# Eight taps per convolution column of the second token half: from VectorE to ScalarE and accumulating DMAs of GpSimd

## Chip, cores and metric

The kernel runs on one NeuronCore of a Trainium2 chip. The metric is the device time of one execution in microseconds; the median of three runs of the kernel before is 3363.21 us (3360.95 to 3363.67).

## What is computed

The reference is a stack of transformer blocks on 1024 tokens of width 1024. Only the first mixer matters here. Its first branch makes `a_val * sigmoid(a_gate)` (512 channels), puts it through a causal depthwise convolution of 31 taps, a layer norm and a SiLU; the second branch is a gated linear recurrence; both are joined and multiplied by `w_out`:

```python
CONV_WIDTH = 31
ya = jax.nn.silu(layer_norm(causal_depthwise_conv(a_val * jax.nn.sigmoid(a_gate), conv_w, conv_b),
                            cnorm_g, cnorm_b))
yb = rg_lru(causal_depthwise_conv(b_rec, lru_conv_w, lru_conv_b), w_a, b_a, w_x, b_x, lru_lambda) \
    * jax.nn.gelu(b_gate)
return jnp.concatenate([ya, yb], axis=-1) @ w_out
```

After it come a layer norm, a SwiGLU feed-forward, differential attention with its own feed-forward, and a second block (mLSTM and Fourier mixing, another feed-forward). Everything is float32; a matrix product is done as three products of a high and a low part.

## The kernel before

Activations lie with channels on the 128 partitions and tokens along the free dimension. The 512 channels of the first branch are four **columns** c of 128 channels; the 1024 tokens are two **halves** h of 512. For column c, `ga[c]` holds the gated values and `co[c]` the convolution's sum, both 128 x 1024 float32 in SBUF.

`mixer_even` (L411) goes through the columns. `a_proj(c)` (L459) multiplies the weights on TensorE, ScalarE takes the gate from PSUM through a sigmoid (L463) and VectorE multiplies the value in (L466). `conv(c, h)` (L481) is the convolution of one half: ScalarE begins it with tap 0 and the bias (L483), then 30 VectorE instructions (L487) each add one shifted, scaled copy of `ga[c]` to `co[c]` in place. For half 0 these are 511 to 482 elements long, for half 1 always 512. In the same loop (L549 to L558) `r_proj`, `taps` (L506) and `lru` (L509) make the recurrence of column c; `lru` multiplies on TensorE (L515) into two PSUM buffers that ScalarE empties with sigmoids (L516). The loop calls `conv(c, 0)` for each column, but the second halves, `conv(c, 1)`, stand only after the pipeline of the first four token tiles (L630 to L632).

That pipeline is `prep0` (L573: transpose the four `co` columns of a tile of 128 tokens on TensorE, L576; mean and variance on VectorE; the inverse root on GpSimd, L261 and L262; normalise on VectorE, L579), `prep1` (L581: transpose back, L584; SiLU on ScalarE, L587) and the products with `w_out` (L592, L565). A second pipeline (L634) does tiles 4 to 7, which need the second halves of all four columns, and starts the feed-forward (`start`, L770).

The order on each engine is not the order of the calls. A list scheduler fixes it when the kernel is built: it takes at each moment the instruction called earliest among those whose inputs and buffers are ready by its cost estimates. So second-half taps, called late, are put as fill into VectorE's free moments from the start. At run time each engine goes through its own list strictly in order and waits where an input isn't there. Buffers come from pools; `self.tmp` (L204) gives 128 x 512 buffers of which there are three, and a fourth waits until the first was released by its last reader. GpSimd issues no DMA in the kernel before; all are issued on SyncE's queue.

Of the kernel before, what the change touches and what calls it, by code (L numbers as in the profile page):

```python
# [14 lines left out]
ALU = mybir.AluOpType  # L15
AX = mybir.AxisListType
P = 128
S = 1024
# [3 lines left out]
H512 = 512  # L22
# [32 lines left out]
TS, TS0, TSM, T2 = True, False, True, 3  # L55
SE, SO, S2, S3, S4 = 1, 0, 1, 0, 1
NC1 = 0
EY = 2
W0 = 0
HA = 1  # L60
# [25 lines left out]
def half(h):  # L86
    return slice(h * H512, (h + 1) * H512)


def blk(i):  # L90
    return slice(i * P, (i + 1) * P)
# [70 lines left out]
class Net:  # L162
# [248 lines left out]
    def mixer_even(self, xr, xn, start):  # L411
        nc, A = self.nc, self.A
# [3 lines left out]
        for h in range(2):  # L416
            r = self.rp.tile([P, KT, P], F32, tag="raw", name=self.name("raw"))
            w0.append([self.wp.tile([P, KT, P], F32R, tag="w", name=self.name("w0")) for _ in range(2)])
            for k in range(0, KT, 2):
# [4 lines left out]
                t = self.u("xt", (P, 2, H512))  # L424
# [28 lines left out]
        ga = [self.u("ga") for _ in range(4)]  # L453
        co = [self.u("co") for _ in range(4)]
# [4 lines left out]
        def a_proj(c):  # L459
            g = ga[c]  # L460

            def gate(p, h):
                nc.scalar.activation(g[:, half(h)], p, AF.Sigmoid, bias=self.c("b_in", 4 + c))  # L463

            def val(p, h):
                nc.vector.scalar_tensor_tensor(g[:, half(h)], p, self.c("b_in", c), g[:, half(h)],  # L466
                                               op0=ALU.add, op1=ALU.mult)

            if c > 0:
                proj(4 + c, gate)  # L470
                yield
                proj(c, val)
                return
            yield
            for h in range(2):
                for w, evac in zip(w0, (gate, val)):
                    p = self.pa("pi")
                    self.feat(p, w, x, h)
                    evac(p, h)

        def conv(c, h):  # L481
            lo_, hi_ = h * H512, (h + 1) * H512
            nc.scalar.activation(co[c][:, lo_:hi_], ga[c][:, lo_:hi_], AF.Identity, bias=self.c("conv_b", c),  # L483
                                 scale=self.c("conv_w", 31 * c + 30))
            for s in range(1, 31):
                a = max(lo_, s)
                nc.vector.scalar_tensor_tensor(  # L487
                    co[c][:, a:hi_], ga[c][:, a - s:hi_ - s], self.c("conv_w", 31 * c + 30 - s),
                    co[c][:, a:hi_], op0=ALU.mult, op1=ALU.add)

        def r_proj(c):
            rec = recs[c] = self.u("rec")

            def evr(p, h):
                nc.scalar.activation(rec[:, half(h)], p, AF.Identity, bias=self.c("b_in", 12 + c))

            proj(12 + c, evr)
# [3 lines left out]
        def taps(c):  # L501
            rec = recs[c]
            rc = rcs[c] = self.u("rc")
            nc.scalar.activation(rc, rec, AF.Identity, bias=self.c("lconv_b", c), scale=self.c("lconv_w", 4 * c + 3))
            for s in range(1, 4):
                nc.vector.scalar_tensor_tensor(rc[:, s:], rec[:, :S - s], self.c("lconv_w", 4 * c + 3 - s),  # L506
                                               rc[:, s:], op0=ALU.mult, op1=ALU.add)

        def lru(c):  # L509
            rec, rc = recs[c], rcs[c]  # L510
            r, ig, a = self.u("r"), self.u("ig"), self.u("a")
            for h in range(2):
                for j, (dst, b) in enumerate(((r, "b_a"), (ig, "b_x"))):
                    p = self.pb("pg")[:, 0:H512]
                    nc.tensor.matmul(p, wg[:, 4 * j + c, :], rc[:, half(h)], start=True, stop=True)  # L515
                    nc.scalar.activation(dst[:, half(h)], p, AF.Sigmoid, bias=self.c(b, c))  # L516
            nc.scalar.activation(a, r, AF.Exp, scale=ca[:, 4 + c:5 + c])
            nc.scalar.activation(r, r, AF.Tanh, scale=ca[:, c:c + 1])
            nc.vector.tensor_mul(ig, ig, rc)
            nc.scalar.activation(rc, a, AF.Square)  # L520
            nc.vector.scalar_tensor_tensor(r, rc, 1.0, r, op0=ALU.add, op1=ALU.mult)
            nc.scalar.activation(r, r, AF.Sqrt)
            nc.vector.tensor_mul(ig, ig, r)
            nc.vector.tensor_tensor_scan(rec, a, ig, 0.0, op0=ALU.mult, op1=ALU.add)
# [3 lines left out]
        def g_steps(cs):  # L528
            ws = [self.weight(A["w_in0"][8 + c], pool=8 + c in W0P) for c in cs]
            gs = [self.u("gel") for c in cs]  # L530
            for h in range(2):
                for c, w, g in zip(cs, ws, gs):
                    p = self.pa("pi")
                    self.feat(p, w, x, h)
                    nc.scalar.activation(g[:, half(h)], p, AF.Gelu_apprx_tanh, bias=self.c("b_in", 8 + c))
                    if h == 1:
                        nc.vector.tensor_mul(g, g, recs[c])
                        hi, lo = self.u("ybh", dt=F32R), self.u("ybl", dt=F32R)
                        self.split(hi, lo, g)
                        yb.append((hi, lo))  # L540
                    yield

        def run(g):
            for _ in g:
                pass

        run(a_proj(0))
        conv(0, 0)
        for c in range(4):  # L549
            r_proj(c)  # L550
            taps(c)
            g = a_proj(c + 1) if c < 3 else g_steps((0,))
            if EV:
                next(g, None)
            lru(c)
            run(g)
            if c < 3:
                conv(c + 1, 0)  # L558
        def rows_b(p, i, first, last):
            for h in range(2):  # L560
                for c in range(4):
                    self.mm3(p[:, half(h)], (yb[c][0][:, blk(i)], yb[c][1][:, blk(i)]),
                             (wb[0][:, c, half(h)], wb[1][:, c, half(h)]), first and c == 0, last and c == 3)

        def prod_b(i):  # L565
            p = self.pb("yo")
            rows_b(p, i, True, True)
            nc.vector.scalar_tensor_tensor(xr[i], xr[i], DN_ALPHA, p, op0=ALU.mult, op1=ALU.add)
# [38 lines left out]

        for c in range(NC1):
            conv(c, 1)
# [20 lines left out]
        self.pipe(pre + [(2, prod_ab), (2, lambda i: prod_b(i + 4)), (3, norm)], range(4))  # L630
        for c in range(NC1, 4):
            conv(c, 1)  # L632
# [698 lines left out]
    def block2_mix(self, x, xr, xn, start):  # L1331
# [370 lines left out]
        def gather(i):  # L1702
            og = self.u("og", (P, 4, P))
            nc.sync.dma_start(og, ogd[:, :, blk(i)].rearrange("h p t -> p h t"))
            if i < 4:
                yf = [[yfs[k // 2][l][:, k % 2, blk(i)] for k in range(4)] for l in range(2)]
            else:
                t = self.y_tile()
                for a in range(2):
                    self.split(*(t[l][:, 2 * a:2 * a + 2, :] for l in range(2)), y2s[a][:, :, blk(7 - i)][:, :, ::-1])  # L1710
                yf = [[t[l][:, k, :] for k in range(4)] for l in range(2)]
            ys[i] = [yf, og, None]

        def prod_f(i):
            p, y = self.pb("yo"), ys[i][0]
            ys[i][2] = p
            for h in range(2):
                for k in range(4):
                    self.mm3(p[:, half(h)], (y[0][k], y[1][k]),
                             (w[0][0][:, k, half(h)], w[0][1][:, k, half(h)]), k == 0, False)  # L1720
                    if k % 2:
                        yield
# [7 lines left out]
        def early():  # L1730
            for _ in fg:
                yield
            w.append(self.load_w_out(A["w_out2"], 4))
            for i in range(EY):
                gather(i)
            yield
            for i in range(EY):
                yield from prod_f(i)
# [16 lines left out]
        def moments(i):  # L1755
            if i >= EY:
                gather(i)
            mv = self.small("mv4", 8)
            m3 = mv.rearrange("p (h t) -> p h t", t=2)
            hh = [H[h // 2][i // 4][:, i % 4, (h % 2) * P:(h % 2 + 1) * P] for h in range(4)]  # L1760
            for h in range(4):
                st = self.mp.tile([P, 6], F32, tag="bn4", name=self.name("st"), bufs=4)
                nc.vector.bn_stats(st, hh[h])
                nc.vector.bn_aggr(m3[:, h, :], st)
            rs = self.small("rs4", 4)
            self.rsqrt(rs, m3[:, :, 1], 1.0, EPS)
            nm = self.small("nm4", 4)
            nc.vector.scalar_tensor_tensor(nm, m3[:, :, 0], -1.0, rs, op0=ALU.mult, op1=ALU.mult)
            ys[i].append((nm, rs, hh))
            xr.append(self.u("xr"))  # L1770
            nc.sync.dma_start(xr[i], spill[blk(i), :])
# [258 lines left out]
```

## Time and profile before

| | us |
|---|---|
| median of 3 runs | 3363.21 |
| the profiled execution, its own time | 3360.71 |
| its span (first to last instruction) | 3358.9 |
| TensorE (PE) busy | 3245.6 |
| VectorE (DVE) busy | 2195.7 |
| ScalarE (ACT) busy | 1389.4 |
| GpSimd (POOL) busy | 226.3 |

PE is matmul, DVE VectorE, ACT ScalarE, POOL GpSimd, SP SyncE. Times in rows count from the start of the span. A timeline merges like instructions that follow each other: a row gives start, length, instruction, tile written <- tiles read, how many, and in brackets the idle time before it with what ended it. A waits row says who waited for whom, the total, the count and the longest. A stretch row gives the stretch, its length, and per engine the busy time with the number of instructions. Line numbers are those of the kernel before.

### The profile page before, as it was taken

Reading aid. Unit: us, or ns where it says so; the run is one execution under the profiler, and the core shown is the slowest. Engines: PE = TensorE matmul, PEld = TensorE weight load, DVE = VectorE, ACT = ScalarE, POOL = GpSimd, SP = SyncE. Lnnn points to the kernel's source line nnn. Section 1 sums busy time; section 2 is a strip of 40 time slices with the busy share of each in tenths; the row PEclk is TensorE's granted clock in tenths of the full one; section 3 lists DMA queues with packets and bytes.
Section 4 is the critical chain, followed back from the end, with each engine's and each line's share of the span. In section 5 each row is a group of like instructions: output and inputs, shape, how many; then the busy total and the mean of one; then the engine's idle time right before and its main releaser. Section 6 shows DMA issues by size and latency. Waiting matters only on the chain. (4 is left out here: it accounts for less than half of the span.)

```text
span 3358.9 us, 40965 instructions
## 1 busy us (share of the span) xinstructions
PE 3245.6 (97%) x15588; PEld 2688.4 (80%) x15588; DVE 2195.7 (65%) x3474; ACT 1389.4 (41%) x2402; POOL 226.3 (7%) x417
## 2 busy tenths in 40 slices
PE   8998999999999999999999999999999999999998
PEld 7777788888878888877788888788777878888887
DVE  8998855555457777676765558654346986675535
ACT  4554433332137777663533331234335454442111
POOL 1011000000010111111000000023001200000001
PEclk9999999999999999999999999999999999999999
DMA  3131322234222111151332238621123333354312
GB/s 127 44 113 63 108 87 76 91 130 161 84 74 98 54 32 51 41 157 60 119 110 91 99 131 296 200 89 68 57 76 116 110 129 118 112 183 161 105 50 80
DMA packets 191765, 348.69 MB, mean 104 GB/s; under 512 B 14384, under 2 KB 105936, under 8 KB 191568
## 3 DMA queue, kind: packets, MB, share of 16 engines
q1 hardware_dynamic: 191568, 346.07, 31.0%
q8 instruction: 123, 2.02, 0.2%
q14 instruction: 74, 0.61, 0.1%
HBM read 268.41 MB, written 72.36 MB: 101 GB/s over the span
## 5 line engine op out<-in xcount | busy, mean ns | idle before, releaser
L214 ACT CAST wh<-raw 128x1024 fp32r<-128x1024 f32 (+1 forms) x275 | 282.7, 1047 | 330.4 <-DVE raw L677 131.3
L215 DVE TENSOR_TENSOR wl<-raw,wh 128x1024 fp32r<-128x1024 f32 (+1 forms) x275 | 330.2, 1217 | 111.6 <-ACT wh L214 107.4
L214 ACT CAST ht<-ht 128x512 fp32r<-128x512 f32 (+1 forms) x168 | 97.2, 579 | 534.9 <-DMA ht<-hd 511.5
L236 PE MATMUL dn<-wd,ht 128*128 128x512 f32 x704 | 274.0, 389 | 0.8 <-ACT wd L214 0.8
L237 PE MATMUL dn<-wd,ht 128*128 128x512 f32 x704 | 274.0, 389 | 0.6 <-DVE wd L215 0.6
L238 PE MATMUL dn<-wd,ht 128*128 128x512 f32 x704 | 273.9, 389 | 0.0
L215 DVE TENSOR_TENSOR ht<-ht 128x512 fp32r<-128x512 f32 (+1 forms) x168 | 106.6, 638 | 171.4 <-ACT ht L214 170.3
L236 PE MATMUL dn<-wh,ht 128*128 128x512 f32 x512 | 201.6, 394 | 8.1 <-DVE xr L901 6.8
L238 PE MATMUL dn<-wh,ht 128*128 128x512 f32 x512 | 200.4, 391 | 0.1
L237 PE MATMUL dn<-wl,ht 128*128 128x512 f32 x512 | 200.2, 391 | 0.0
L236 PE MATMUL wx<-bh,wh 128*128 128x512 f32 x480 | 189.2, 394 | 5.0 <-ACT keep L693 3.7
L238 PE MATMUL wx<-bh,wl 128*128 128x512 f32 x480 | 187.5, 392 | 1.1 <-DVE wl L215 1.1
L237 PE MATMUL wx<-bl,wh 128*128 128x512 f32 x480 | 187.9, 392 | 0.0
L236 PE MATMUL pi<-xh,wh 128*128 128x512 f32 x416 | 166.8, 401 | 4.3 <-ACT wh L214 4.3
L237 PE MATMUL pi<-xl,wh 128*128 128x512 f32 x416 | 165.8, 399 | 0.0
L487 DVE SCALAR_TENSOR_TENSOR co<-ga,col,co 128x512 f32<-128x512 f32 (+21 forms) x240 | 164.2, 738 | 1.1 <-ACT co L483 0.9
L238 PE MATMUL pi<-xh,wl 128*128 128x512 f32 x416 | 164.7, 396 | 0.0
L236 PEld LDWEIGHTS dn<-wd,ht 128*128 128x128 f32 x704 | 132.1, 188 | 28.9 <-ACT wd L214 1.2
L237 PEld LDWEIGHTS dn<-wd,ht 128*128 128x128 f32 x704 | 132.1, 188 | 28.3 <-DVE wd L215 1.0
L288 POOL TENSOR_SCALAR nm<-sum 128x1 f32<-128x1 f32 x47 | 18.2, 388 | 2023.8 <-DVE xr L901 1304.1
L238 PEld LDWEIGHTS dn<-wd,ht 128*128 128x128 f32 x704 | 132.1, 188 | 27.5
L236 PEld LDWEIGHTS dn<-wh,ht 128*128 128x128 f32 x512 | 96.8, 189 | 29.6 <-issue 6.9
(456 smaller groups left out, 8368.7 us busy)
## 6 DMA issues: line engine op xcount, KB each, us to landing
raw<-w_gu SPq DMA_DIRECT2D x100, 512.0 KB
hd<-g SPq DMA_DIRECT2D x152, 256.0 KB
raw<-w_f SPq DMA_DIRECT2D x70, 512.0 KB
ht<-hd SPq DMA_DIRECT2D x136, 256.0 KB
raw<-w_ada SPq DMA_DIRECT2D x48, 512.0 KB
raw<-w_dn SPq DMA_DIRECT2D x44, 512.0 KB
raw<-w_in SPq DMA_DIRECT2D x26, 512.0 KB
raw<-w_out SPq DMA_DIRECT2D x24, 512.0 KB
```

The costliest lines, as they stand in the source:

```text
L214: self.nc.scalar.copy(hi, src)
L215: (self.nc.gpsimd if pool else self.nc.vector).tensor_sub(lo, src, hi.bitcast(F32))
L236: mm(out, l[0], r[0], start=first, stop=False, **kw)
L237: mm(out, l[0], r[1], start=False, stop=False, **kw)
L238: mm(out, l[1], r[0], start=False, stop=last, **kw)
L288: (nc.vector if NMV else nc.gpsimd).tensor_scalar(nm, a, -1.0 / D, None, op0=ALU.mult)
L487: nc.vector.scalar_tensor_tensor(co[c][:, a:hi_], ga[c][:, a - s:hi_ - s], self.c("conv_w", 31 * c + 30 - s), co[c][:, a:hi_], op0=ALU.mul ...
```

## The change

A constant `NFAR = 8` is added. The ScalarE instruction that begins a half is now a function of its own, `first`. For half 1 it is called by `far(c)`, at the end of column c's turn in the loop, right behind `conv(c + 1, 0)`. `far(c)` then takes the eight farthest taps (30 to 23): ScalarE multiplies the shifted copy of `ga[c]` by the tap's weight into a `tmp` buffer, and a DMA issued by GpSimd adds that buffer to the second half of `co[c]` in SBUF. Each of these DMAs writes the same 128 x 512 elements, so each must follow the one before. `conv(c, 1)` keeps its place and does taps 1 to 22 on VectorE, in place, after the DMAs.

```diff
+NFAR = 8
@@
-        def conv(c, h):
+        def first(c, h):
             lo_, hi_ = h * H512, (h + 1) * H512
             nc.scalar.activation(co[c][:, lo_:hi_], ga[c][:, lo_:hi_], AF.Identity, bias=self.c("conv_b", c),
                                  scale=self.c("conv_w", 31 * c + 30))
-            for s in range(1, 31):
+
+        def far(c):
+
+            first(c, 1)
+            for s in range(30, 30 - NFAR, -1):
+                t = self.tmp("far")
+                nc.scalar.mul(t, ga[c][:, H512 - s:S - s], self.c("conv_w", 31 * c + 30 - s))
+                nc.gpsimd.dma_start(co[c][:, half(1)], t, accum_op=ALU.add)
+
+        def conv(c, h):
+            lo_, hi_ = h * H512, (h + 1) * H512
+            if h == 0:
+                first(c, h)
+            for s in range(1, 31 - h * NFAR):
                 a = max(lo_, s)
                 nc.vector.scalar_tensor_tensor(
                     co[c][:, a:hi_], ga[c][:, a - s:hi_ - s], self.c("conv_w", 31 * c + 30 - s),
@@
             if c < 3:
                 conv(c + 1, 0)
+            far(c)
```

## Rows read from the trace of the kernel before

**Rows 1.** The page's head and part 1: busy time, share and instructions.

```profile
span 3358.9 us, 40965 instructions
...
PE 3245.6 (97%) x15588; PEld 2688.4 (80%) x15588; DVE 2195.7 (65%) x3474; ACT 1389.4 (41%) x2402; POOL 226.3 (7%) x417
```

**Rows 2.** Stretches of the span: busy time (count) by engine, clock, DMA share, GB/s.

```profile
core 0: us, PE busy (x) PEld busy (x) DVE busy (x) ACT busy (x) POOL busy (x), PEclk, DMA share, GB/s
20.00:66.00 46.00, 46.00 (x196) 36.51 (x196) 42.01 (x56) 19.49 (x22) 0.00 (x0) 1.00 0.25 83
66.00:160.00 94.00, 94.00 (x401) 74.67 (x400) 94.00 (x122) 52.35 (x57) 0.00 (x0) 1.00 0.12 38
160.00:200.00 40.00, 37.00 (x149) 27.69 (x147) 39.06 (x50) 22.67 (x25) 0.00 (x0) 0.96 0.16 45
200.00:280.00 80.00, 75.82 (x349) 62.11 (x349) 76.77 (x110) 28.37 (x43) 12.54 (x20) 1.00 0.38 138
280.00:294.00 14.00, 2.00 (x13) 1.39 (x11) 12.45 (x21) 2.55 (x5) 1.48 (x4) 0.62 0.10 39
```

**Rows 3.** Waits of PE between 30 and 340 us: total, times, longest us.

```profile
PE pt L576 <- DVE co L487: 9.2, 2, 8.9
PE pt L584 <- DVE t L579: 5.5, 2, 3.1
PE pg L515 <- DVE rc L506: 2.7, 1, 2.7
```

**Rows 4.** Timeline of PE, 278 to 298 us: start, us, instructions [idle before].

```profile
280.39 0.49 PE L576 MATMUL pt<-ident,co 128*128 128x128 f32 x3
289.77 0.69 PE L576 MATMUL pt<-ident,co 128*128 128x128 f32 x2 [8.90 <-DVE co L487]
293.57 1.09 PE L584 MATMUL pt<-ident,t 128*128 128x128 f32 x4 [3.11 <-DVE t L579]
...
296.96 0.60 PE L584 MATMUL pt<-ident,t 128*128 128x128 f32 x4
```

**Rows 5.** Timeline of DVE, 284 to 294 us, around the last tap.

```profile
288.97 0.74 DVE L487 SCALAR_TENSOR_TENSOR co<-ga,col,co 128x512 f32<-128x512 f32 x1
```

**Rows 6.** Stretches, taps of line 487 alone: busy time and count.

```profile
20.00:36.00 16.00, 6.27 (x9) 1.00 0.40 138
36.00:66.20 30.20, 23.10 (x36) 1.00 0.16 53
...
sum 270.00, DVE 164.20; mean DVE 32.84
```

**Rows 7.** Timeline of DVE, 60 to 72 us: column 0's last first-half tap.

```profile
66.13 0.71 DVE L487 SCALAR_TENSOR_TENSOR co<-ga,col,co 128x482 f32<-128x482 f32 x1
```

**Rows 8.** Line 483 on ACT: ns min/median/max, first and last start.

```profile
L483 ACT ACTIVATE co<-ga,col x8: 815/817/818, 24.7 to 145.4; 128x512 f32<-128x512 f32 x8
```

**Rows 9.** Timeline of ACT, 30 to 40 us: column 0's second-half start.

```profile
34.02 0.81 ACT L483 ACTIVATE co<-ga,col 128x512 f32<-128x512 f32 x1
```

**Rows 10.** Timeline of ACT, 54 to 66 us: the sigmoids of column 0.

```profile
56.23 0.68 ACT L516 ACTIVATE r<-pg,col 128x512 f32<-128x512 f32 x1
...
58.13 0.69 ACT L516 ACTIVATE r<-pg,col 128x512 f32<-128x512 f32 x1 [0.64 <-PE pg L515]
```

**Rows 11.** Issue of 256 KB loads on SP at 723.95 us, their first reader.

```profile
723.95 0.93 SPq L834 DMA_DIRECT2D ht<-hd  x2
...
727.37 0.62 ACT L214 CAST ht<-ht 128x512 fp32r<-128x512 f32 x1 [2.59 <-DMA ht<-hd]
```

**Rows 12.** One 256 KB store issued at 340.93 us: GB/s in 0.1 us slices.

```profile
GB/s 0 0 0 0 0 0 0 0 164 369 430 389 369 348 389 164 0 0 0 0 0 0 0 0 0 0 0 0 0 0 0 0 0 0 0 0 0 0 0 0
```

**Rows 13.** Timeline of POOL, 20 to 210 us: its first work after the start.

```profile
200.17 0.60 POOL L261 TENSOR_SCALAR rs<-mv 128x1 f32<-128x1 f32 x1 [180.75 <-DVE mv L271]
```

**Rows 14.** Timeline of PE, 159 to 170 us: a shorter wait and the clock.

```profile
163.25 3.24 PE L515 MATMUL pg<-rc,wg 128*128 128x512 f32 x4 [2.71 <-DVE rc L506]
...
168.10 1.88 PE L515 MATMUL pg<-rc,wg 128*128 128x512 f32 x4
```

## The prediction

> **What bounds the kernel now.** I read the page's head and part 1 first: TensorE is busy 3245.6 of 3358.9 us [rows 1]. So a microsecond counts only where TensorE idles, and the convolution lies in the first 300 us. The table of stretches shows where [rows 2]: TensorE is full from 20 to 160 us, then loses 3.0 us up to 200 and 4.2 up to 280, and from 280 to 294 it works 2.0 of 14 us. VectorE is as full as it can be (94.0 of 94, 39.1 of 40, 76.8 of 80), ScalarE about half full (52.4 of 94), GpSimd empty until 200. The waits of TensorE name the cause [rows 3]: 9.2 us for `co` of line 487, the convolution, 5.5 for the normalised tile of line 579, 2.7 for `rc` of line 506, all made by VectorE. The timeline shows the large one [rows 4]: TensorE has transposed `co` of the first columns by 280.88 us and stands 8.90 us until the last; VectorE's last tap runs from 288.97 to 289.71 [rows 5]. A second wait of 3.11 us follows, while the tile's statistics are made, and the granted clock of the stretch is 0.62 [rows 2, 4]: part of it at the lower level, 1.2 instead of 2.4 GHz. So VectorE's list up to the last tap sets when the second token half can begin.
>
> **What is removed.** 240 taps take VectorE 164.20 us, 0.684 each [rows 6]. Four columns by eight taps leave: 32 x 0.684 = 21.9 us.
>
> **What that cover was.** Second-half taps are fill. By 66.2 us 9 + 36 = 45 taps had begun [rows 6], of which 30 are column 0's first half, whose last starts at 66.13 [rows 7]; so 15 second-half taps, 10.3 us, filled VectorE before column 1 came in. Now the remaining taps of column 0 must follow eight DMAs. ScalarE begins that half at 34.02 [rows 9] and needs 0.82 us for it and, I take it, as much for each multiplication (same engine, same 128 x 512 from SBUF to SBUF) [rows 8]; the first product is there at about 35.65.
>
> **One accumulating DMA** is not in the trace; call its time T, from one landing to the next. The nearest rows are plain transfers of 256 KB: one issued at 723.95 had its reader waiting until 727.37, 3.4 us with its landing [rows 11]; in another the bytes themselves move for 0.8 us [rows 12]. Bounds: below, 2.2 us (issue to last byte of the store is 1.6 [rows 12], and I put some 0.6 for the landing); above, 6.8, as if reading, adding and writing were two plain transfers in turn. I take 4.0, one transfer's 3.4 with most of its bytes moved once more, nearest to the row that has a landing in it. Chain 0 then ends at 35.65 + 8 x 4.0 = 67.7, so the 15 taps of fill are lost and VectorE idles instead.
>
> The Trainium skill has a price too: "DMA: Bandwidth & Descriptors", section "Anatomy of one DMA — SWDGE (gpsimd) path", gives about 2.0 us plus the bytes at 436 GB/s for a DMA that GpSimd issues, by which this one is an estimated 2.6 us; the row's 3.4 us is of SyncE's queue and another route, so no run here decides between them. By that price chain 0 would end near 56.5 us and the time would be near that of the first rival below.
>
> **VectorE, net.** 21.9 less 10.3 is 11.6 us. From 66 us on it was full, so its last tap ends near 289.7 - 11.6 = 278.1, before TensorE's 280.88. The 8.90 us wait goes: **-8.9**. The 3.11 us wait stays; it is now the late thing, statistics to transposes. The low clock I count at **-0.6**: four transposes took 1.09 us in it and 0.60 after it [rows 4], but a gap of 2.71 us at 160 was also followed by slow products, 3.24 against 1.88 [rows 14], so the remaining gap may keep some; ends 0 and -1.4.
>
> **ScalarE** gets 32 x 0.82 = 26 us. It had 26.5 us free from 20 to 66, 41.7 to 160 and 17.3 to 200 [rows 2], so most hides there. What may not hide is one multiplication standing ahead of a sigmoid of `lru`: the third sigmoid waits 0.64 us for its product [rows 10], and that product waits for a buffer of the first. Ends: 0, and 4 columns x 2 x 0.82 = 6.6; I take **+1.5**, near one half of 4 x 0.82, since half the engine's time is free.
>
> **Queues.** Nothing is added to SyncE's. GpSimd gets 32 DMAs, each waiting for a product and for the DMA before it; behind them stands the inverse root of the first tile, which ran at 200.17 after 180.75 us of nothing [rows 13]. Columns end their values about 37 us apart (34.02 to 145.4 in three steps [rows 8, 9]) and a chain is 32 us, so the fourth ends at 145.4 + 1.6 + 32 = 179; the root is late only from T = 6.7 on. The DMA engines have room (shares 0.25 and 0.12 [rows 2]): nothing. ScalarE waits as well: with three buffers, multiplication 4 waits for DMA 1 and multiplication 8 for DMA 5; behind it stand the casts of weights and the sigmoids of the column. That is free while T is near what the scheduler assumed, and the second rival is about it.
>
> **Sum:** -8.9 - 0.6 + 1.5 = -8.0, so 3352.7 against the profiled execution's 3360.7. That execution is 2.5 under the median of 3363.2; the forecast is for the median, **3355.2**.
>
> **Rivals.**
> *More is gained.* If T is near 3 or less, chain 0 ends before 60, some of the fill comes back, and the last tap moves up to 10 us further ahead. Then the statistics can run beside the products too: -8.9 - 3.1 - 1.4, and the 2.7 us wait at 160 may go with its 1.4 us of low clock; with 1.5 for ScalarE -16.0, near 3347. For it: the store's short 1.6 us; against: the adding reads twice and GpSimd must issue.
> *Slower: ScalarE is held by its own DMAs.* If multiplication 8 stands ahead of the sigmoids in ScalarE's list and T is longer than the scheduler assumed, the sigmoids wait. Multiplication 8 ends at 35.65 + 5T + 0.82, the first sigmoid started at 56.23 [rows 10]: late by 5T - 19.8. TensorE stands in its line behind the pair of PSUM buffers, so four columns cost 4 x (5T - 19.8); this eats the 8.0 at T = 4.4. At T = 5.0 it is 20.8 - 8.0, so 3376; at 6.8 some 49 us. For it: ScalarE's list is strictly in order and TensorE has no idle time from 20 to 160 to give. Against: the sigmoids' columns are served last, the scheduler may have put multiplications behind them, where only casts made early wait.
> *Gained and given back.* T between about 4.2 and 4.6 at the same place, or the last `co` transposes now wait on another late VectorE instruction instead of the taps: within 6 us of before, 3363. That the change does not take VectorE's work away can't be: the 32 instructions are gone from its list; that the chain comes so late that the taps of column 3 wait for it needs it to end after some 240 us, T over 11.
>
> **Chances.** The forecast's case 0.42 (own range 3349 to 3360), more gained 0.17, given back 0.22, slower 0.19. A measurement here can tell about 0.2% from no change, 6.7 us, so 3356.5 and 3369.9 are the bounds. Faster: 0.17, and four fifths of 0.42, 0.34: 0.51. Same: 0.08 of the forecast's case, 0.18 of the given back: 0.26. Slower: 0.19 and 0.04: 0.23. The range takes in the first rival's 3347 with a little below it for waits at 200 us, and reaches to 3373 at the other end, T just under 5, so that the far part of the slower case and the best of the gains are left out: 3343 to 3373.
>
> **What would show it.** Right: 208 taps on line 487 of before, about 142 us; VectorE idle for some 10 us between 36 and 67; the last tap near 278; TensorE's wait for `co` at 281 gone and about 3 us for the tile of line 579 left; 32 DMAs on GpSimd's queue some 4.0 us apart within a column. Wrong: TensorE waits in lines 515 or 236 between 50 and 160 us that it did not have; ScalarE idle ahead of a multiplication, released by a DMA; GpSimd's first root later than 200 us; or the wait for `co` as long as before.

## The result and the profile after

| | before | after |
|---|---|---|
| median, us | 3362.08 (4 runs) | 3379.26 (4 runs) |
| profiled execution: time / span, us | 3360.71 / 3358.9 | 3379.17 / 3377.3 |
| first `wx` product (next stage) at, us | 324.3 | 341.6 |

The changed kernel is slower: ratio 1.0051, 95% interval 1.0039 to 1.0062, some 17 us. The forecast was 3355.2 with a range of 3343 to 3373; both the sign and the range were wrong. The page's part 1 of the kernel after (busy time by engine) shows work removed as meant: VectorE 17 us less, ScalarE 21 and GpSimd 29 more [rows 1].

```profile
PE 3255.5 (96%) x15588; PEld 2694.2 (80%) x15588; DVE 2178.3 (64%) x3442; ACT 1410.1 (42%) x2434; POOL 255.7 (8%) x449
```

Where the time went, by landmarks: the product rows of two lines of TensorE, the recurrence's `pg` and the next stage's `wx`, with the first and last start in us. First before:

```profile
L515 PE MATMUL pg<-rc,wg x32: 590/592/1057, 54.7 to 169.4; 128*128 128x512 f32 x32
L236 PE MATMUL wx<-bh,wh x480: 389/389/796, 324.3 to 2987.6; 128*128 128x512 f32 x160
```

The same two after:

```profile
L529 PE MATMUL pg<-rc,wg x32: 591/784/1193, 57.3 to 192.9; 128*128 128x512 f32 x32
L237 PE MATMUL wx<-bh,wh x480: 387/389/796, 341.6 to 3004.8; 128*128 128x512 f32 x160
```

The recurrence begins 2.6 us late and ends 23.5 us late; the next stage begins only 17.3 late, and its last product is 17.2 late. So more than 23 us were lost up to 193 us, a part was won back before 341, and nothing changes behind that. The stretches after, with the columns of [rows 2], say the same:

```profile
20.00:66.00 46.00, 43.19 (x177) 33.47 (x176) 33.44 (x41) 20.91 (x27) 6.36 (x7) 0.96 0.47 120
66.00:160.00 94.00, 80.69 (x316) 61.31 (x315) 82.58 (x106) 53.39 (x63) 14.93 (x17) 0.91 0.37 81
160.00:200.00 40.00, 37.42 (x151) 28.83 (x150) 36.35 (x48) 26.53 (x31) 7.01 (x8) 0.96 0.37 77
280.00:294.00 14.00, 14.00 (x64) 11.58 (x63) 8.55 (x11) 1.24 (x2) 0.85 (x2) 1.00 0.42 150
```

TensorE, full between 20 and 160 us before, now loses 2.8 and 13.3 us there; the 12 us it lost from 280 to 294 are gone. Its waits from 30 to 340 us (who for whom, total, times, longest):

```profile
PE pg L529 <- DVE rc L520: 15.9, 3, 8.3
PE pt L599 <- DVE t L594: 5.3, 2, 2.8
PE pg L529 <- issue: 2.8, 1, 2.8
...
PE pt L591 <- DVE co L501: 0.3, 1, 0.3
```

The wait for `co` fell from 9.2 to 0.3 us, as forecast [rows 3]. In its place stands `rc`, the recurrence's own short convolution. What made it late is read from the second column's turn, backwards. First GpSimd's timeline (column 0's chain: the first two and the last of its eight DMAs), where one issue takes 0.88 us:

```profile
35.41 1.09 POOL L493 DMA_DIRECT2D co<-far  x1 [15.93 <-ACT far L492]
41.11 0.88 POOL L493 DMA_DIRECT2D co<-far  x1 [4.61 <-DMA co<-far]
...
66.18 0.89 POOL L493 DMA_DIRECT2D co<-far  x1 [4.15 <-ACT a L531]
```

VectorE's timeline, 50 to 106 us: it comes to the second half's first remaining tap at 62.0 and stands 7.37 us until the eighth DMA has landed. Behind that tap, in its list, stand the other seven taps of the row, then `ig` of the recurrence and `ga` of column 1, now at 75.59 and 76.72:

```profile
60.82 1.22 DVE L216 TENSOR_TENSOR wl<-raw,wh 128x1024 fp32r<-128x1024 f32 x1
69.41 6.26 DVE L501 SCALAR_TENSOR_TENSOR co<-ga,col,co 128x512 f32<-128x512 f32 x8 [7.37 <-DMA co<-far]
75.59 1.22 DVE L533 TENSOR_TENSOR ig<-ig,rc 128x1024 f32<-128x1024 f32 x1
76.72 0.74 DVE L467 SCALAR_TENSOR_TENSOR ga<-pi,col,ga 128x512 f32<-128x512 f32 x1
...
98.59 1.28 DVE L520 SCALAR_TENSOR_TENSOR rc<-rec,col,rc 128x1023 f32<-128x1023 f32 x1 [1.87 <-ACT rc L518]
```

ScalarE's timeline, 30 to 112 us, carries that on. It waits 8.28 us for `ig`; its two evacuations of `rec` (line 509) begin at 86.31 and 94.39; and between the two it stands for its own DMAs, because the product three back must have been added before its buffer is free:

```profile
76.84 1.06 ACT L534 ACTIVATE rc<-a 128x1024 f32<-128x1024 f32 x1 [8.28 <-DVE ig L533]
...
86.31 0.66 ACT L509 ACTIVATE rec<-pi,col 128x512 f32<-128x512 f32 x1
88.92 0.73 ACT L492 ACTIVATE far<-ga,col 128x512 f32<-128x512 f32 x1 [1.95 <-DMA co<-far]
92.82 0.73 ACT L492 ACTIVATE far<-ga,col 128x512 f32<-128x512 f32 x1 [3.18 <-DMA co<-far]
...
94.39 0.68 ACT L509 ACTIVATE rec<-pi,col 128x512 f32<-128x512 f32 x1
96.70 0.72 ACT L492 ACTIVATE far<-ga,col 128x512 f32<-128x512 f32 x1 [1.63 <-DMA co<-far]
97.33 1.23 ACT L518 ACTIVATE rc<-rec,col 128x1024 f32<-128x1024 f32 x1
```

In the kernel before the same four instructions, two of VectorE's and two of ScalarE's, began 11 to 13 us earlier:

```profile
63.70 1.21 DVE L519 TENSOR_TENSOR ig<-ig,rc 128x1024 f32<-128x1024 f32 x1
65.47 0.74 DVE L466 SCALAR_TENSOR_TENSOR ga<-pi,col,ga 128x512 f32<-128x512 f32 x1
...
74.88 0.69 ACT L495 ACTIVATE rec<-pi,col 128x512 f32<-128x512 f32 x1 [3.41 <-PE pi L238]
81.06 0.68 ACT L495 ACTIVATE rec<-pi,col 128x512 f32<-128x512 f32 x1
```

After the change VectorE can make `rc` only behind the second of these evacuations (98.59 above), and TensorE, which has done all that stands ahead of it in its list by 95.4, starts at 103.70. Its timeline, and then the stretches of the gap and behind it (columns of [rows 2]):

```profile
103.70 3.75 PE L529 MATMUL pg<-rc,wg 128*128 128x512 f32 x4 [8.34 <-DVE rc L520]
```

```profile
95.00:104.00 9.00, 0.66 (x3) 0.33 (x2) 7.13 (x8) 4.62 (x6) 1.77 (x2) 0.72 0.59 133
104.00:112.00 8.00, 8.00 (x18) 4.13 (x18) 8.00 (x13) 5.68 (x8) 1.74 (x2) 0.68 0.46 105
```

The gap costs twice: behind it the granted clock is 0.68, so for part of the stretch 1.2 instead of 2.4 GHz. By that row it takes an estimated 0.32 x 8 = 2.6 us more, though TensorE is busy without a break.

The first gap, 2.81 us ahead of column 0's `pg` at 57.34, comes before VectorE's stand and is ScalarE's: two of its products waited 2.51 and 3.07 us for DMAs, so that the second evacuation of `rec`, behind them in its list, began at 48.88 instead of 44.82.

Two stands (places where an engine waits for a DMA with other work behind it in its list) are thus visible on the same chain at once, and both are large in the list of waits, 30 to 340 us:

```profile
ACT far L492 <- DMA co<-far: 45.6, 19, 4.3
...
ACT rc L534 <- DVE ig L533: 13.2, 3, 8.3
DVE co L501 <- DMA co<-far: 11.5, 2, 7.4
```

### The profile page after: what moved, and what is told of

It reads as the page before. It is cut to its first block, busy times and chain, and to the rows that moved or that the text cites. A ratio compares the mean times of both kernels' runs of the same rounds, so it can differ in the third digit from the quotient of the medians.

```text
span 3377.3 us, 41056 instructions
## 1 busy us (share of the span) xinstructions
PE 3255.5 (96%) x15588; PEld 2694.2 (80%) x15588; DVE 2178.3 (64%) x3442; ACT 1410.1 (42%) x2434; POOL 255.7 (8%) x449
## 4 chain that ended last, share of the span: by engine, by line
PE 68%; DVE 8%; ACT 5%; DMA 5%; issue 2%; POOL 2%; SPq 0%; POOLq 0%; DVEq 0%; ACTq 0%
PE dn L237 6%; PE dn L239 6%; PE dn L238 6%; PE wy L238 4%; PE wy L239 4%; PE wy L237 4%; PE wz L237 3%; PE wz L238 3%; PE wz L239 3%; PE wx L237 3%; PE wx L239 3%; PE wx L238 3%; PE po L1116 2%; PE pi L237 1%; PE pi L238 1%
## 5 line engine op out<-in xcount | busy, mean ns | idle before, releaser
L216 DVE TENSOR_TENSOR ht<-ht 128x512 fp32r<-128x512 f32 (+1 forms) x168 | 106.8, 638 | 169.3 <-ACT ht L215 167.9
L238 PE MATMUL dn<-wl,ht 128*128 128x512 f32 x512 | 199.7, 390 | 0.0
L501 DVE SCALAR_TENSOR_TENSOR co<-ga,col,co 128x512 f32<-128x512 f32 (+22 forms) x208 | 143.9, 735 | 13.4 <-DMA co<-far 11.5
```

What stands on the lines that cost most here:

```text
L216: (self.nc.gpsimd if pool else self.nc.vector).tensor_sub(lo, src, hi.bitcast(F32))
L238: mm(out, l[0], r[1], start=False, stop=False, **kw)
L501: nc.vector.scalar_tensor_tensor(co[c][:, a:hi_], ga[c][:, a - s:hi_ - s], self.c("conv_w", 31 * c + 30 - s), co[c][:, a:hi_], op0=ALU.mul ...
```

## The experiments

Three theories stood against each other, named in the expectations: **V**, VectorE stands in its list for a chain's last DMA, with `ig` and `ga` behind it; **H**, ScalarE is held by its own DMAs, with `rec`, `rc` and casts behind it; **M**, the plain time of the 32 multiplications. Every variant has its engine lists made anew by the scheduler, so a variant can differ in order as well. All runs, in the order of the text (pg: start of the recurrence's last product; wx: start of the next stage; both of the profiled execution, which was 6 us over its median for "DMAs, no products", 5 over for "four taps, own buffers", 8 under for "four taps, again" and within 3 for the others; the ratio is to the kernel before, run beside it):

| variant | pg | wx | median, us | ratio (95%) |
|---|---|---|---|---|
| before | 169.4 | 324.3 | 3362.1 | |
| after | 192.9 | 341.6 | 3379.3 | 1.0051 (1.0039 to 1.0062) |
| products, no DMAs | 169.8 | 315.5 | 3354.7 | 0.9980 (0.9970 to 0.9989) |
| DMAs, no products | 187.3 | 335.1 | 3368.5 | 1.0019 (1.0010 to 1.0028) |
| own buffers | 176.4 | 330.7 | 3369.5 | 1.0029 (1.0017 to 1.0042) |
| not in column 0 | 174.9 | 319.8 | 3358.6 | 0.9989 (0.9979 to 0.9998) |
| column 0 with a sum of its own | 187.3 | 333.0 | 3369.3 | 1.0023 (1.0014 to 1.0033) |
| all with sums of their own | 184.3 | 333.2 | 3370.3 | 1.0029 (1.0018 to 1.0040) |
| the same, and own buffers | 171.2 | 323.0 | 3362.3 | 1.0006 (0.9997 to 1.0016) |
| the same, not in column 3 | 173.1 | 316.9 | 3354.4 | 0.9976 (0.9965 to 0.9986) |
| issued late | 166.3 | 432.5 | 3469.0 | 1.0325 (1.0310 to 1.0341) |
| two taps | 174.7 | 322.5 | 3357.7 | 0.9990 (0.9981 to 0.9999) |
| four taps | 167.5 | 312.9 | 3349.9 | 0.9972 (0.9961 to 0.9984) |
| four taps, again | 167.9 | 313.5 | 3352.1 | 0.9967 (0.9956 to 0.9979) |
| four taps, four buffers | 170.4 | 315.2 | 3353.7 | 0.9968 (0.9956 to 0.9981) |
| four taps, own buffers | 174.6 | 329.0 | 3363.4 | 1.0003 (0.9994 to 1.0013) |
| six taps | 181.5 | 327.0 | 3364.2 | 1.0003 (0.9994 to 1.0012) |

### Products without DMAs

```diff
                 nc.scalar.mul(t, ga[c][:, H512 - s:S - s], self.c("conv_w", 31 * c + 30 - s))
-                nc.gpsimd.dma_start(co[c][:, half(1)], t, accum_op=ALU.add)
```

> The 32 multiplications stay, their 32 DMAs are left out, so eight taps of the second half are not added. Theories H and V both lose their wait: 3350 to 3356, below the kernel before by the 8 us forecast for VectorE's relief and possibly the 3 us of statistics. Theory M (the multiplications alone delay the sigmoids and casts): 3362 or more.

Measured 3354.7, with `wx` at 315.5, 8.8 us ahead of before. That is the forecast's relief (8.9 us), and it holds with all 32 multiplications in ScalarE's list: M falls as the cause of the loss. The loss is in the DMAs and in who waits for them. This kernel is no lower bound, though: one with 16 multiplications and their DMAs is faster still (four taps, below), and whether the other multiplications or the order of the lists make that difference was not separated.

### DMAs without products

```diff
-                t = self.tmp("far")
-                nc.scalar.mul(t, ga[c][:, H512 - s:S - s], self.c("conv_w", 31 * c + 30 - s))
-                nc.gpsimd.dma_start(co[c][:, half(1)], t, accum_op=ALU.add)
+                nc.gpsimd.dma_start(co[c][:, half(1)], ga[c][:, H512 - s:S - s], accum_op=ALU.add)
```

> The multiplications are left out and the DMAs add the shifted gated values themselves, so the chain has no partner on ScalarE: the computation lacks the eight weights. Theory H: as with own buffers, 3360 to 3367, since nothing of ScalarE waits for a DMA. Theory M: faster than with own buffers by 4 us or more. Theory V: chain 0 runs at its bare pace, 34 + 8 x 3.9 = 65 us, so VectorE still stands some 3 us there, less than the 7.4; time 3365 to 3372.

Measured 3368.5. ScalarE waits for no DMA here, and still 13.8 of the 24.6 us remain that lie between the kernel without DMAs and the changed one (medians; by `wx` of the slower profiled execution, 19.6 of 26.1). The waits, 30 to 340 us:

```profile
DVE co L499 <- DMA co<-ga: 18.3, 2, 10.2
PE pg L527 <- DVE rc L518: 16.6, 3, 9.3
```

V without H is enough to make the kernel slower. The size expected for it (3 us in column 0) was wrong: VectorE stands 10.2 and 8.1 us, longer than in the kernel after. The two stands are not separate prices that add up: with ScalarE free, VectorE is sooner at the same chain (57.96 instead of 62.04 us).

### Own buffers

```diff
+                if s % 2 == 0:
+                    pair = self.u("far")
-                t = self.tmp("far")
+                t = pair[:, half(s % 2)]
```

> Eight products of a column get eight buffers of their own, so ScalarE no longer waits for the DMA three products back; the chain of eight DMAs and VectorE's taps behind it stay. Theory H (ScalarE is held in order by its own DMAs, 45.6 us of waits, and that makes the recurrent taps late for TensorE): those waits go to near 0, TensorE's 15.9 us of waits for rc fall under 6, time 3362 to 3368. Theory V (VectorE's list stands at the second-half taps until a chain's last DMA, 7.4 + 4.1 us, with ig and ga behind): that wait stays within 2 us and the time stays at 3373 or more. Theory M (the plain work of 32 multiplications): as after, 3379.

Measured 3369.5, ten less than after; neither H's 3362 to 3368 nor V's 3373 was met. It separates less than intended: the new lists have column 0's products behind its recurrence, so that the first DMA is issued at 67 instead of 35 us. VectorE's stand is there still, 7.9 us long, at 90 to 98 us, when chain 0 now ends; TensorE's waits for `rc` fell from 15.9 to 9.1 us; and a new wait of 10.3 us for a normalised tile came up, of the kind that is told below for GpSimd.

### Not in column 0

```diff
-            if h == 0:
+            if h == 0 or c == 0:
                 first(c, h)
-            for s in range(1, 31 - h * NFAR):
+            for s in range(1, 31 - (h * NFAR if c else 0)):
@@
-            far(c)
+            far(c) if c else None
```

> Column 0 keeps all its 30 second-half taps on VectorE; columns 1 to 3 as changed. Theory V (the stand of VectorE for chain 0, which sets column 1 back by 11 us): the time falls to 3364 to 3370. Theory H (ScalarE is held in each column alike): only column 0's 2.8 us gap with its low clock goes, 3374 or more, and the gaps of 8.3, 5.0 and 2.6 us in columns 1 to 3 stay.

Measured 3358.6, below even V's 3364, and the kernel is no slower than before. Leaving out column 0's chain alone thus takes away 20.7 of the 24.6 us (21.8 of 26.1 by `wx`). In the list of its waits VectorE has none for a DMA any more, while ScalarE's are still long:

```profile
ACT far L492 <- DMA co<-far: 29.9, 14, 5.3
...
PE pg L529 <- DVE rc L520: 4.1, 3, 1.6
```

The kernel is 4 us behind the one without DMAs, so 29.9 us of waiting on ScalarE cost far less than their sum. They are not free: TensorE waits 4.1 us for `rc` and 5.5 for the sigmoids of line 530, against 2.7 for `rc` alone without DMAs. That fits V, and that VectorE with column 0's 30 taps as fill has other work until each later chain has ended. But column 0's chain holds both stands, so the next run was needed.

### Column 0 with a sum of its own

```diff
             first(c, 1)
+            to = co[c][:, half(1)]
+            if c == 0:
+                to = fas[0] = self.mp.tile([P, H512], F32, tag="fa", name=self.name("fa"), bufs=1)
             for s in range(30, 30 - NFAR, -1):
-                t = self.tmp("far")
+                t = to if c == 0 and s == 30 else self.tmp("far")
                 nc.scalar.mul(t, ga[c][:, H512 - s:S - s], self.c("conv_w", 31 * c + 30 - s))
-                nc.gpsimd.dma_start(co[c][:, half(1)], t, accum_op=ALU.add)
+                if c or s < 30:
+                    nc.gpsimd.dma_start(to, t, accum_op=ALU.add)
@@ conv
+            if h == 1 and c == 0:
+                nc.vector.tensor_add(co[c][:, half(1)], co[c][:, half(1)], fas[0])
```

> Column 0's chain adds to a sum of its own (2 KB more per partition), joined to co by one addition on VectorE that stands some 40 us later in its list; columns 1 to 3 as changed. ScalarE's multiplications of column 0, their holds of three buffers and the DMAs from 35 us on stay. Theory V (VectorE's stand of 7.4 us in front of ig and ga, and the lost fill, carry column 0's loss): 3358 to 3365, near the kernel without column 0's chain. Theory H (ScalarE's holds in column 0 carry it): 3372 or more.

Measured 3369.3, between the two expectations. Column 0 is now on time (`pg` of column 0 at 54.5 us) with its multiplications and holds in place, and the kernel is 10 us faster than after: that is what taking VectorE's stand out of column 0 gains, net of the stands that take its place. The rest did not go. VectorE, with eight taps less to fill in, stands at column 1's chain instead, and ScalarE's holds are seen at TensorE directly. The waits, 30 to 340 us:

```profile
DVE co L507 <- DMA co<-far: 7.1, 1, 7.1
PE pg L537 <- ACT r L538: 5.1, 2, 3.6
PE pg L537 <- ACT far L497: 4.7, 1, 4.7
```

How the 10.7 us between this kernel and the one without column 0's chain divide between V in column 1 and H was not separated.

### Sums of their own in all columns, then own buffers too

```diff
+            if c % 2 == 0:
+                fa[0] = self.u("fa")
+            fas[c] = fa[0][:, half(c % 2)]
             for s in range(30, 30 - NFAR, -1):
-                t = self.tmp("far")
+                t = fas[c] if s == 30 else self.tmp("far")
                 nc.scalar.mul(t, ga[c][:, H512 - s:S - s], self.c("conv_w", 31 * c + 30 - s))
-                nc.gpsimd.dma_start(co[c][:, half(1)], t, accum_op=ALU.add)
+                if s < 30:
+                    nc.gpsimd.dma_start(fas[c], t, accum_op=ALU.add)
@@ conv
+            if h == 1:
+                nc.vector.tensor_add(co[c][:, half(1)], co[c][:, half(1)], fas[c])
```

> The first product is the start of a sum of its own, seven DMAs add the other products to that, and VectorE's 22 taps run on co without a chain behind them; one addition on VectorE joins the two at the end (4 more of 0.7 us). ScalarE still waits for a buffer three products back. Theory V (VectorE's stand for a chain is most of the loss): 3355 to 3362, no wait of VectorE for a DMA over 2 us before 200 us. Theory H (ScalarE's holds alone are most of it): 3368 or more, ScalarE's waits for DMAs still over 30 us in all and TensorE's waits for rc over 10.

Measured 3370.3. No tap stands for a DMA any more (in the list of waits VectorE has none), ScalarE's waits for them are 32.8 us, and TensorE loses 7.9 us to the sigmoids of line 538 and 6.5 to `rc`: H carries this one, as its expectation of 3368 said, though `rc` alone stays under the 10 us expected of it. The second kernel takes the products' buffers from `u` as well, as in the own-buffers run:

> As the sum of its own, and the products have buffers of their own too, so that neither ScalarE nor VectorE stands for a DMA before the join. V and H together explain all of the loss: 3352 to 3358, the time of the kernel whose DMAs were left out (3354.7). If something else of the DMAs costs (their bytes, GpSimd's issue, slower SBUF access of the other engines): 3362 or more, with longer taps or casts than 0.65 and 1.04 us.

Measured 3362.3, better by 8, with `pg` only 1.8 us late; but 7.6 us remain to the kernel without DMAs. The number is that of "something else of the DMAs costs", the cause given with it is not: the median tap takes 740 ns here and 741 in the kernel without DMAs. GpSimd's timeline, 165 to 250 us, has a third stand instead. As with own buffers alone, the lists have the first product late, so that the first DMA is issued at 68.0 us and the last at 215.2, and column 3's chain reaches into GpSimd's next work. The inverse root of the first tile, whose input was ready at 199.7 (VectorE's line 272), waits in GpSimd's list behind an issue that itself waits for the DMA before:

```profile
205.52 0.87 POOL L501 DMA_DIRECT2D fa<-far  x1 [4.92 <-DMA fa<-far]
206.46 0.19 POOL L262 TENSOR_SCALAR rs<-mv 128x1 f32<-128x1 f32 x1
```

and TensorE, in its timeline, stands for the tile:

```profile
208.30 1.09 PE L609 MATMUL pt<-ident,t 128*128 128x128 f32 x4 [7.08 <-DVE t L604]
```

### The same, not in column 3

```diff
-            far(c)
+            if c < 3:
+                far(c)
@@ conv
-            for s in range(1, 31 - h * NFAR):
+            for s in range(1, 31 - (h * NFAR if c < 3 else 0)):
```

> As the sum of its own with buffers of its own (3362.3), but column 3 keeps its 30 taps on VectorE, so that GpSimd has no accumulating DMA left when the first tile's inverse root comes. Theory G (in that kernel the loss had moved to GpSimd: its root stood at 206.5 behind DMA issues of chain 3, and TensorE 7.1 us for the normalised tile): the root runs before 202 us, that wait falls to 3 us, time 3351 to 3357. If the stay at 3362 has another cause (bytes, longer taps): 3360 or more.

Measured 3354.4. GpSimd's last DMA is issued at 172.8 and the root runs at 202.77, when its input comes (not quite before 202, as expected); TensorE's wait for the tile is 2.4 us. The third stand is confirmed, and the kernel reaches the 3354.7 of the one without DMAs, although VectorE still stands once, 4.8 us at column 0's joining addition. The 21 DMAs left here, their bytes and issues, cost nothing that shows. In the kernel after, where the chains begin at 35 us, this third stand plays no part.

### Issued late

```diff
             if c < 3:
                 conv(c + 1, 0)
-            far(c)
@@
         for c in range(NC1, 4):
+            far(c)
             conv(c, 1)
```

> The same 32 products and DMAs, but issued in the program right ahead of the second half's taps, behind the first pipeline, so that they rank behind all of columns 0 to 3 when the order of each engine is made. Theories H and V: what they cost depends on what stands behind the waiting instruction; behind the columns' work nothing of TensorE's does, so TensorE's waits for rc fall to 3 us as in the kernel before and the time to 3354 to 3362, unless chain 3 ends after 270 us and co is waited for again at 281 (then 3362 to 3370). If the loss lies in the DMAs themselves: 3375 or more.

Measured 3469.0, far outside. The first part came: the recurrence is on time (`pg` at 166.3, ahead of before). But ranked behind everything, column 0's first DMA is issued at 272.6 us and the last at 377 us, and TensorE waits for `co` itself (waits, 30 to 460 us):

```profile
PE pt L590 <- DVE co L501: 120.1, 4, 47.5
```

A chain must start early and end before it is needed; nothing between was tried, nor a scheduler that is given the measured time of these DMAs.

### Two, four and six taps

```diff
-NFAR = 8
+NFAR = 2      (and 4, and 6)
```

> NFAR 4: four taps a column instead of eight, otherwise as changed. VectorE loses 16 x 0.68 = 10.9 us of taps, still more than the 8.9 us wait at 281. Theory V: chain 0 ends near 34.4 + 4 x 4.4 = 52 us, before VectorE comes to its taps in earnest, so its stand is under 3 us: 3354 to 3361. Theory H: one buffer wait a column instead of five: 3356 to 3363. If any use of these DMAs costs by itself, half the loss stays: 3366 or more.

> NFAR 4 once more, three buffers, for an interval beside the kernel before on the same chip: 3348 to 3352, ratio 0.996 to 0.9985.

> NFAR 2. Relief theory (the gain is VectorE's taps before 281 us, 0.68 each, up to the 8.9 us wait): 8 x 0.68 = 5.5 of the 8.9 us gained, some 3 us of the wait for co left: 3354 to 3358, between the kernel before and the one with four (3349.9). If the gain with four came from elsewhere (another order of the engines' lists): no relation, 3349 or 3362.

> NFAR 6. A threshold (chain 0 must end before VectorE comes to its taps near 62 us; 34.4 + 6 x 4.4 = 61): 3349 to 3358. A price per DMA, on a line from four (3349.9) to eight (3379.3): 3362 to 3367. ScalarE's waits for DMAs between the 10.9 of four and the 45.6 of eight in either case.

Four taps: 3349.9 and 3352.1 in two sittings, faster than the kernel before by some 0.3% and than the one after by some 0.8%, and faster than either theory had expected (3354 to 3363). In the waits, 30 to 340 us, VectorE has none for a DMA, and ScalarE's are short and hidden:

```profile
ACT far L492 <- DMA co<-far: 10.9, 4, 4.4
...
PE pg L529 <- DVE rc L520: 3.0, 2, 2.7
```

Two taps gave 3357.7, as the relief theory had it: a wait of 3.0 us for `co` is left. But even so short a chain left a stand: the list has the first remaining tap earlier, and VectorE waits 4.0 us there for the second DMA, until 45.67. Six gave 3364.2, on the line from four to eight, and not the 3349 to 3358 of a threshold that V alone would set. There VectorE stands only 2.6 us, but TensorE's `pg` waits in all four columns; its timeline:

```profile
57.46 1.19 PE L529 MATMUL pg<-rc,wg 128*128 128x512 f32 x1 [3.09 <-issue]
98.93 1.52 PE L529 MATMUL pg<-rc,wg 128*128 128x512 f32 x3 [2.11 <-DVE rc L520]
139.24 2.04 PE L529 MATMUL pg<-rc,wg 128*128 128x512 f32 x2 [3.95 <-DVE rc L520]
177.00 1.52 PE L529 MATMUL pg<-rc,wg 128*128 128x512 f32 x3 [2.72 <-DVE rc L520]
```

ScalarE's waits for DMAs are 32.2 us there, and `rc` is begun late on it. With six taps H can carry most of the loss, since V has little to carry it with.

### Four taps with more buffers

```diff
-    def tmp(self, name, bufs=3):
+    def tmp(self, name, bufs=4):
```

(the same in the two other places that give the pool's size), and, as a kernel of its own, four taps with the buffers of the own-buffers run.

> NFAR 4 and one more buffer for products (four), so ScalarE waits for no DMA of its own column. If the 10.9 us that ScalarE waited with four taps and three buffers still delay TensorE: 3344 to 3348. If they hide: 3348 to 3352, as with three buffers. Slower only if another order of the lists opens a wait of its own, which TensorE's waits before 300 us would show.

> NFAR 4 and four buffers of their own, so that ScalarE waits for no DMA. If the 10.9 us that ScalarE waits with four taps still delays anything of TensorE: 3344 to 3348. If those waits hide: as with four, 3348 to 3352.

With four buffers ScalarE waits for no DMA at all and the time is no better, 3353.7 (3349.9 and 3352.1 with three): at four taps H is hidden. With buffers from `u` it is 3363.4, against both expectations: the lists again have the first product late (first DMA at 66.9 us), and TensorE in the profiled execution waits 6.9 us for `co` and 6.6 for normalised tiles. What a variant does to the order of the lists weighs as much as the wait that it was made to remove.

## Why the prediction was wrong, by its own steps

**Removed work, right.** 208 taps are left, 143.9 us in the stretches (142 forecast). The relief at the end came: the wait for `co` went from 9.2 to 0.3 us, and of the 23.5 us of delay at 193 us 17.3 are left at 341.6; without DMAs the gain is 8.8 against the 8.9 forecast.

**T, nearly right.** Forecast 4.0 us from landing to landing and chain 0's end at 67.7. The DMA's landing comes 3.3 us after the start of its issue (median of 32; 3.2 to 5.1), issues follow at 3.85 us where nothing comes between (44.90 to 48.76 to 52.61), and the chain ended at 69.4. Over all of chain 0, with the waits between ScalarE's products and GpSimd's issues, the pace was (66.18 - 35.41) / 7 = 4.4, just the T at which the second rival has the gain eaten up. The Trainium skill, "DMA: Bandwidth & Descriptors", section "Anatomy of one DMA — SWDGE (gpsimd) path", gives about 2.0 us plus the bytes at 436 GB/s, by which this DMA is an estimated 2.6 us; that is 0.7 us under the 3.3 measured for these accumulating DMAs, and the measurement decides.

**The lost fill, right in size, wrong in price: the step that failed.** The step "so the 15 taps of fill are lost and VectorE idles instead" was charged against VectorE's last tap alone, 10.3 of 21.9 us. VectorE did lose 8.6 us of work between 20 and 66. But an engine that works its list in order does not idle for free: it stood in front of a tap that was not urgent, with `ig` and `ga` behind it, on which TensorE's next column hung. The prediction asked who is behind GpSimd's and ScalarE's new waits and not who is behind VectorE's. Taking that one stand away gained 10 us (the run with a sum of its own for column 0), and the kernel in which VectorE stands and ScalarE waits for no DMA is 14 us behind the one without DMAs (the run without products).

**ScalarE +1.5, wrong.** It was priced at its multiplications' time, 26 us in 85 free ones, and the kernel without DMAs, which has all of them and gains 8.8 us, shows no cost of it (a multiplication is 0.72, not 0.82 us). What costs something are the holds, 45.6 us of waits, though not in full. The prediction named them, called them free while T is near the scheduler's assumption, and made them its second rival. How the loss divides between VectorE's stand and these holds stays open.

**The slow rival, 0.19: nearest in time (3376), partly right in mechanism.** The first sigmoid is late by 5T - 19.8 = 2.2 us at T = 4.4; measured 59.46 - 56.23 = 3.2. The near agreement is in part luck: multiplication 8 began at 56.74, earlier than its formula, and two evacuations and a cast stood between it and the sigmoid. The holds cost something in the runs with six taps and with sums of their own, where VectorE hardly stands. But it multiplied the sigmoid's delay by four columns, while behind the holds it was `rec`, `rc` and the casts that came late; and it had no word on VectorE. Two of the signs that the prediction named for being wrong did come: new waits of TensorE at `pg`, and ScalarE idle ahead of a multiplication until a DMA has landed.

**The low clock, wrong in sign.** One gap went, at 281 us, but at `pg` there are four instead of one, 2.81, 8.34, 4.97 and 2.58 us, and the granted clock of the stretch from 66 to 160 fell from 1.00 to 0.91. Behind the first, third and fourth gap of the kernel after the stretches are these:

```profile
57.30:66.00 8.70, 8.66 (x24) 5.21 (x25) 4.60 (x6) 7.11 (x10) 1.74 (x2) 0.80 0.57 121
147.70:156.00 8.30, 8.28 (x17) 4.42 (x18) 8.30 (x13) 5.60 (x8) 1.77 (x2) 0.65 0.54 125
186.80:196.00 9.20, 9.20 (x26) 5.78 (x27) 9.20 (x14) 6.95 (x9) 1.76 (x2) 0.81 0.53 117
```

and behind the one gap of the kernel before this:

```profile
163.20:172.00 8.80, 8.75 (x24) 5.26 (x25) 8.80 (x13) 4.18 (x5) 0.00 (x0) 0.81 0.21 60
```

By these clocks, and the 0.68 above, the low clock takes an estimated 9.0 us after and 1.7 before, 7.3 more. The gaps themselves are 18.7 us against 2.7, 16.0 more. Together that is 23.3 of the 23.5 us by which the recurrence ends late, so nearly a third of the delay is low clock. The prediction had the pattern in its rows [rows 14] and priced it only for gaps that it already had, not for new ones.

**GpSimd's root, right for this kernel**: the last DMA was issued at 198.0 and the root ran at 223.7, when its input came, so it waited for no DMA. (The fourth chain ended near 201 instead of the forecast 179, because its column came late.) But the place was the right one to ask about: in the variant with sums and buffers of their own it was the stand that was left.

## To carry to other kernels

A chain of dependent DMAs put through in-order engines costs what stands behind each waiting instruction, so price every new wait on every list that the chain touches, the one that consumes its result first, and not only the sum of work removed. When the chain takes nearly as long as the loop's period (here 34 us from first issue to last landing, of 36), removing one stand moved the wait to the next engine; shortening the chain to four taps (17 us) left none that TensorE saw. An engine freed on average can still be late where it matters.

## What was not expected of the hardware

An accumulating DMA of 256 KB from SBUF to SBUF takes GpSimd 0.88 us to issue and lands 3.3 us after the start of the issue (medians of 32). VectorE and ScalarE are not visibly slowed beside them: the median tap is 736 ns against 741 before, and the median cast of a weight up to 340 us (line 215; 214 before) 1.03 us against 1.05. Behind TensorE's longest gap, 8.34 us, the granted clock was 0.68 over 8 us of full work, so that by estimate this gap cost 2.6 us, some three tenths, over its length.
